# Two feed forwards' openings: an order each for ScalarE and VectorE, and low halves moved from GpSimd to VectorE

## The chip, the cores and the metric

The kernel runs on one core of a Trainium2 chip. The metric is the device time of one execution in microseconds; before, the median of three runs is 1371.8 us.

## The reference

Two transformer blocks run one after the other on 512 tokens of width 1024, in fp32. Each ends with a gated feed forward of inner width 2816, and the change concerns these two alone:

```python
# block 1
x = x + rms_norm(mixed, norm_mix_post)
h = rms_norm(x, norm_ffn_pre)
f = (silu(h @ w_gate) * (h @ w_up)) @ w_down
x = x + rms_norm(f, norm_ffn_post)
# block 2
x = x + merged @ w_out
h = rms_norm_2(x, norm_ffn)
x = x + (silu(h @ w_ffn_gate) * (h @ w_ffn_up)) @ w_ffn_down
```

`rms_norm(x, g)` is x / sqrt(mean(x²) + eps) * g over the 1024 columns of a token.

## The kernel before, in words

**Arithmetic.** TensorE multiplies in a reduced fp32 form, so each operand is split into a high and a low half, and a product takes three matmuls (`mm3`, or the three pairs in `prod`). A split is one ScalarE copy (the high half) and one subtraction (the low half), on VectorE or, where `split_from` is given `lo_eng`, on that engine. Splits of 1024 columns are made by `w8`, of 512 by `w4`; their results stand in the profile as `wt` and `u`.

**The feed forward.** `ffn` (L440) runs over 22 tiles of 128 inner columns. Per tile it takes products of quarter blocks in the manner of Strassen's scheme: instead of the four quarters of the tokens' matrix X and of the weights, it multiplies sums of them. The left sums of X (`s2`, `s3`, `p1`, `p4` and the quarter `a22`) are made once; the weights' sums are made in every tile by four GpSimd additions of 512 columns in place (`Tile.sums`, L397 to L400), on the raw tiles `G` (of w_gate) and `U` (of w_up) as they were loaded. From the sums come `wb` (the split of `U`) and `wa` (of `G`).

**An opening.** The left sums need the last two token tiles, which are not ready when the feed forward starts. So `ffn` first runs an opening: for the first 12 tiles of the first feed forward and the first 8 of the second ("heads"), it computes the gate products with the quarters that are there, `a11` (`first`) and `a12` (`second`). Its parts carry names: "L5" loads and splits tile 5's gate weights, "E5" copies out its first product (ScalarE), "S5" its silu (ScalarE). With these are woven, in the first feed forward, the norms of the token tiles 2 and 3 (`norm_fill`, "sq2", "rs2", "post2", "add2", "sq'2", "rs'2", "pre2", and the same with 3; "rs" is a reciprocal root of nine VectorE instructions, "sq" and "sq'" mean squares on ScalarE), then the left sums' subtractions, "sub0" and "sub1" (four VectorE subtractions of 512 columns each), and ten left blocks, "b0" to "b9": four TensorE transposes, two ScalarE high halves and two VectorE low halves, which the profile shows as `sh<-tp`. Two PSUM buffers take the transposes, so the third block waits for the first to be split. Within a tile's norm, `pre` writes what the left blocks transpose. Behind the opening stands the loop over all 22 tiles, whose first products are with `s2`.

**What sets the order.** The instructions of the parts are recorded by `noted` in `bag`; a string of names (`ORDER1` at L1062, `ORDER2` at L1388) then chains each engine's instructions in the order of the names through `behind` (L289), one string for both engines. TensorE is chained by `prod` and `left_block` as the code is written. Behind the chain, L527 splits the first tile's sums: high halves of `wb` and `wa` on ScalarE, low halves on GpSimd (they are the `wt` instructions of L255 on POOL). Then tile 1 is loaded, and its sums and tile 2's follow on GpSimd. All weights are loaded by SP into rotating raw buffers; two of these hold tile 0's `G` and `U` during the opening.

`early` counts the tiles whose gate weights are split by two `w4` instead of one `w8`: 2 in the first feed forward, 0 in the second.

Of the kernel before, what the change touches and what calls it, by code (L numbers as in the profile page):

```python
# [10 lines left out]
BF16 = mybir.dt.bfloat16  # L11
# [6 lines left out]
P = 128  # L18
S = 512
D = 1024  # L20
# [14 lines left out]
def transformer_pair(ctx: ExitStack, tc: tile.TileContext, A: dict, out: bass.AP, spill: dict):  # L35
# [6 lines left out]
    nc = tc.nc  # L42
# [20 lines left out]
    vec, sca = Engine(nc.vector, "dve"), Engine(nc.scalar, "act")  # L63
    bag = {}

    @contextmanager
    def noted(name):
        bags.append(bag.setdefault(name, []))
        yield
        bags.pop()  # L70
# [5 lines left out]
    wt1 = ctx.enter_context(tc.tile_pool(name="wt1", bufs=4))  # L76
# [6 lines left out]
    pl = {}  # L83
# [14 lines left out]
    cnt = [0, 0, 0, 0, 0]  # L98
    loads = []

    def nm(s):
        cnt[0] += 1
        return f"{s}_{cnt[0]}"
# [4 lines left out]
    def t_tile(shape, dt=F32):  # L108
        return pl["t"].tile(shape, dt, tag="t", name=nm("t"))

    def p_tile(shape, dt=F32):
        return pl["p"].tile(shape, dt, tag="p", name=nm("p"))

    def s_tile(n, tag, dt=F32, bufs=6):
        return sm.tile([P, n], dt, tag=tag, name=nm(tag), bufs=bufs)
# [12 lines left out]
    def tp_tile():  # L128
        return ps_tile("tp")
# [14 lines left out]
    def queue_after(later, earlier):  # L144

        tc.add_manual_dep(later.ins, earlier.ins.name,
                          mybir.DependencyInfo(mybir.DependencyClass.NoSync, mybir.DependencyReason.DATA),
                          reason="order")
# [38 lines left out]
            vec.scalar_tensor_tensor(y, t, 1.5, y, op0=ALU.subtract, op1=ALU.mult)  # L187
        return y

    def mean_square(x_ap):  # L190

        junk = (p_tile([P, D], BF16) if "p" in pl else t_tile([P, D], BF16) if "j" not in pl else
                pl["j"].tile([P, D], BF16, tag="j", name=nm("j")))
        ms = s_tile(1, "ms")
        sca.activation(junk, x_ap, AF.Square, scale=1.0 / 32.0, accum_out=ms)
        return ms
# [79 lines left out]
    def w8(src, pool, lo_eng=None):  # L276

        w = pool.tile([P, 2, 1024], F32R, tag="wt", name=nm("wt"))
        split_from(src, w[:, 0], w[:, 1], lo_eng=lo_eng)
        return w  # L280
# [8 lines left out]
    def behind(eng, ins):  # L289

        if eng in queue:
            queue_after(ins, queue[eng])
        queue[eng] = ins
        return ins
# [145 lines left out]
    def ffn(X, wgate, wup, wdown, t0, heads, early, h, order, before_last, second_phase, evac, middle):  # L440
# [14 lines left out]
        both = pl["raws"]  # L455
# [39 lines left out]
        for f in range(heads + 1):  # L495
# [22 lines left out]
            for n in (2 * i, 2 * i + 1):  # L518
                if i >= 0:
                    with noted(f"b{n}"):  # L520
                        late[n]()
        for name in order.split():
            for eng, ins in bag[name]:
                behind(eng, ins)
        bag.clear()
        pl["raws"], cnt[4] = both, 1
        t0.wb, t0.wa = w8(t0.U, wt1, nc.gpsimd), w8(t0.G, wt1, nc.gpsimd)  # L527
        T[1].load()
        T[1].w22 = w4(T[1].U[:, 512:1024])
        T[1].sums()  # L530
# [3 lines left out]
        for f in range(NF):  # L534
            t = T[f]
            n1, n2 = T[f + 1] if f + 1 < NF else None, T[f + 2] if f + 2 < NF else None
            p = n1 if n1 and not n1.head else None
# [104 lines left out]
    x_t = []  # L642
# [67 lines left out]
    for tt in range(NT):  # L710
# [4 lines left out]
        sq = t_tile([P, 2, 64])  # L715
# [12 lines left out]
    for tt in range(NT):  # L728
# [3 lines left out]
        pt = tp_tile()  # L732
# [201 lines left out]
    mixed = {}  # L934
# [31 lines left out]
    def norm_fill(tt):  # L966
        if tt == 0:
            rows[0] = (row_in("norm_mix_post"), row_in("norm_ffn_pre"))
        post_norm_then_pre(vec, mixed[tt], x_t[tt], *rows[0], mean_square, rsqrt, lambda n: noted(f"{n}{tt}"))

    hX = {}

# [5 lines left out]
    rows = [None]  # L978
# [50 lines left out]
    t0 = early_tile(A["w_gate"], A["w_up"])  # L1029
# [28 lines left out]
    def middle1():  # L1058
        hT2.extend(new_hT())
        flush()  # L1060

    ORDER1 = ("L2 L3 sq2 E0 rs2 E1 S0 post2 L4 add2 sq'2 E2 S1 sq3 L5 E3 S2 rs'2 rs3 L6 E4 S3 pre2 post3 L7 E5 S4 "  # L1062
              "add3 sq'3 L8 E6 S5 sub0 L9 E7 S6 rs'3 pre3 L10 E8 S7 b0 b1 sub1 L11 E9 S8 b2 b3 E10 S9 b4 b5 "
              "E11 S10 b6 b7 S11 b8 b9")
    ffn(hX, A["w_gate"], A["w_up"], A["w_down"], t0, 12, 2, mixed, ORDER1, [], down_phase1, evac1, (10, middle1))
    hT = hT2


# [190 lines left out]
    def gate_fill(_):  # L1259
# [3 lines left out]
    order = [[(U, 0)], [(U, 1), (G, 0)], [(Y, 0), (G, 0)], [(U, 2), (Y, 1)],  # L1263
             [(U, 3), (G, 0)], [(Y, 2), (G, 0)], [(G, 0), (Y, 3)], [(G, 0)]]
# [32 lines left out]
    for f2 in range(4):  # L1297
        wb = load_w(A["w_branch_b"][f2])
        for fi in range(2):
            f = 2 * f2 + fi  # L1300
# [16 lines left out]
    t0 = early_tile(A["w_ffn_gate"], A["w_ffn_up"])  # L1317
    hX = left_tiles()
# [30 lines left out]
    x_t = []  # L1349
# [33 lines left out]
    def load_x2():  # L1383
        for tt in (0, 1):
            x_t.append(u_tile([P, D]))
            nc.sync.dma_start(out=x_t[tt], in_=spill["x3"][tt])

    ORDER2 = ("L0 L1 L2 add3 sq3 rs3 E0 pre3 L3 E1 S0 L4 E2 S1 sub0 L5 E3 S2 L6 E4 S3 b0 b1 sub1 L7 E5 S4 b2 b3 "  # L1388
              "E6 S5 b4 b5 E7 S6 b6 b7 S7 b8 b9")
    ffn(hX, A["w_ffn_gate"], A["w_ffn_up"], A["w_ffn_down"], t0, 8, 0, h_t, ORDER2, [load_x2],  # L1390
        down_phase2, evac2, (10, middle2))
    hT = hT3
# [15 lines left out]
    for tt in range(NT):  # L1408
# [17 lines left out]
        n = len(parts) - 1  # L1426
# [15 lines left out]
def post_norm_then_pre(vec, m, xt, g_post, g_pre, mean_square, rsqrt, noted):  # L1442

    with noted("sq"):
        ms = mean_square(m)
    with noted("rs"):
        r = rsqrt(ms, 1)
    with noted("post"):
        vec.scalar_tensor_tensor(m, m, r, g_post, op0=ALU.mult, op1=ALU.mult)
    with noted("add"):  # L1450
        vec.tensor_tensor(xt, xt, m, op=ALU.add)
    with noted("sq'"):
        ms = mean_square(xt)
    with noted("rs'"):
        r2 = rsqrt(ms, 1)
    with noted("pre"):
        scale_rows(vec, m, xt, r2, g_pre)
# [121 lines left out]
```

## Time and profile before

| what | value |
|---|---|
| median of three runs (lowest, highest) | 1371.8 us (1370.57, 1372.34) |
| profiled execution, its own time | 1370.37 us |
| profiled execution, span | 1368.7 us |
| mean granted TensorE clock | 0.993 |
| TensorE busy | 1300.0 us (95%) |
| VectorE busy | 988.0 us (72%) |
| ScalarE busy | 733.2 us (54%) |
| GpSimd busy | 378.9 us (28%) |
| first opening | 229.2 to 289.2 us |
| second opening | 942.7 to 976.3 us |

The span runs from the first to the last instruction in the trace; the execution's own time is 1.7 us longer. Times in the views count from the span's start. Busy shares are means over the whole span and tell little of an opening, which has to be read in order of time. In the trace the operations of parts recorded by `noted` all have the line of the helper, L57, so they are told apart by tile and shape. A matmul's end is modelled, and the starts of two groups in a row give the better measure of how long one took.

### The profile page before, as it was taken

To read this page: it belongs to the slowest core of one execution; us is meant where nothing else is said; L and a number is where in the kernel's file an instruction comes from. 1 tells how busy PE (TensorE), PEld (TensorE's weight loads), DVE (VectorE), ACT (ScalarE), POOL (GpSimd) and SP (SyncE) were. 2 spreads that over 40 slices of the span, in tenths; PEclk is the share of its full clock that TensorE was granted. 3 is DMA by queue.
4 is the path that set the end of the run, shared out by engine and by line. 5 is a ranking of instruction groups with operands and counts; after the bars stand their busy time and mean duration, and the time that the engine had idled before them with its cause. 6 is when DMAs were issued, how large, how long until landed. Compare 5 with 4: busy or idle time off the path is not lost.

```text
span 1368.7 us, 20850 instructions
## 1 busy us (share of the span) xinstructions
PE 1300.0 (95%) x7724; PEld 1108.6 (81%) x7724; DVE 988.0 (72%) x1837; ACT 733.2 (54%) x1333; POOL 378.9 (28%) x367
## 2 busy tenths in 40 slices
PE   8989999789999999999998999989899999999997
PEld 6756667778889999787766778869889999998876
DVE  5889677778887765866886673656788766767665
ACT  6578876634444554544866564534544544544453
POOL 1433222145544341000233010210554344330002
PEclk9999999999999999999999999999999999999999
DMA  8214133434444433833121435553344334437441
GB/s 281 84 32 143 43 106 111 139 119 144 139 139 139 139 109 117 315 126 112 62 78 54 126 133 181 188 212 127 109 151 154 116 117 138 123 108 259 144 138 61
DMA packets 56309, 181.81 MB, mean 133 GB/s; under 512 B 8592, under 2 KB 8976, under 8 KB 56208
## 3 DMA queue, kind: packets, MB, share of 16 engines
q1 hardware_dynamic: 56064, 180.49, 40.2%
q8 instruction: 60, 0.98, 0.3%
q14 instruction: 41, 0.34, 0.1%
q10 hardware_dynamic: 144, 0.00, 0.0%
HBM read 167.88 MB, written 12.58 MB: 132 GB/s over the span
## 4 chain that ended last, share of the span: by engine, by line
PE 61%; DVE 20%; issue 9%; ACT 4%; DMA 3%; POOL 2%; SPq 0%; DVEq 0%; POOLq 0%; ACTq 0%
PE f L349 14%; PE tp L349 9%; PE f L168 5%; PE f L166 5%; PE f L167 5%; DVE t L363 3%; PE acc L166 3%; PE acc L168 3%; PE acc L167 3%; DVE u L363 2%; DVE wt L161 2%; DVE wt L363 1%; PE av L852 1%; DVE p L1196 1%; DVE u L57 1%
## 5 line engine op out<-in xcount | busy, mean ns | idle before, releaser
L349 PE MATMUL tp<-sh,wt 128*128 128x256 f32 x1584 | 205.3, 284 | 3.6 <-DVE sh L57 2.0
L349 PEld LDWEIGHTS tp<-sh,wt 128*128 128x128 f32 x1584 | 197.9, 192 | 11.2 <-DVE t L363 6.4
L360 ACT ACTIVATE wt<-raw 128x1024 fp32r<-128x1024 f32 x152 | 155.6, 1050 | 82.8 <-issue 66.7
L363 DVE TENSOR_TENSOR wt<-raw,wt 128x1024 fp32r<-128x1024 f32 x152 | 190.8, 1255 | 2.0 <-ACT wt L360 1.9
L161 DVE TENSOR_TENSOR wt<-raw,wt 128x1024 fp32r<-128x1024 f32 (+1 forms) x88 | 109.7, 1251 | 50.2 <-ACT wt L160 49.1
L397 POOL TENSOR_TENSOR raw<-raw,raw 128x512 f32<-128x512 f32 x44 | 63.8, 1450 | 289.8 <-DVE wt L363 171.4
L166 PE MATMUL f<-wt,u 128*128 128x512 f32 x280 | 112.2, 402 | 3.9 <-ACT wt L254 2.2
L168 PE MATMUL f<-wt,u 128*128 128x512 f32 x280 | 112.2, 401 | 2.0 <-DVE u L255 2.0
L160 ACT ACTIVATE wt<-raw 128x1024 fp32r<-128x1024 f32 (+1 forms) x88 | 91.3, 1045 | 42.5 <-PE f L168 13.0
L167 PE MATMUL f<-wt,u 128*128 128x512 f32 x280 | 111.3, 398 | 1.4 <-DVE wt L255 1.0
L166 PE MATMUL f<-u,wt 128*128 128x512 f32 x272 | 107.5, 395 | 0.3 <-ACT nx L1097 0.2
L167 PE MATMUL f<-u,wt 128*128 128x512 f32 x272 | 107.0, 393 | 0.0
L168 PE MATMUL f<-u,wt 128*128 128x512 f32 x272 | 106.8, 393 | 0.0
L349 PE MATMUL f<-u,wt 128*128 128x256 f32 x720 | 98.3, 287 | 0.5 <-DVE wt L57 0.5
L349 PEld LDWEIGHTS f<-u,wt 128*128 128x128 f32 x720 | 92.5, 196 | 0.7 <-DVE wt L57 0.7
L363 DVE TENSOR_TENSOR u<-tp,u 128x256 f32<-128x256 f32 x88 | 36.6, 416 | 72.8 <-PE tp L349 72.8
L399 POOL TENSOR_TENSOR raw<-raw,raw 128x512 f32<-128x512 f32 x44 | 57.1, 1297 | 83.9 <-DVE u L363 73.7
L349 PE MATMUL f<-sh,u 128*128 128x256 f32 x528 | 72.0, 286 | 5.0 <-DVE t L363 5.0
L254 ACT ACTIVATE wt<-raw 128x1024 fp32r<-128x1024 f32 x48 | 49.7, 1055 | 45.1 <-PE acc L168 22.0
L349 PEld LDWEIGHTS f<-sh,u 128*128 128x128 f32 x528 | 66.2, 191 | 7.8 <-DVE t L363 7.8
L349 PE MATMUL f<-sh,wt 128*128 128x256 f32 x528 | 70.5, 283 | 0.0
L360 ACT ACTIVATE u<-u 128x256 f32<-128x256 f32 x44 | 18.4, 417 | 95.4 <-DVE u L363 95.4
(335 smaller groups left out, 3043.5 us busy)
## 6 DMA issues: line engine op xcount, KB each, us to landing
raw<-in_w_down SPq DMA_DIRECT2D x44, 512.0 KB, 3.9
raw<-in_w_ffn_down SPq DMA_DIRECT2D x44, 512.0 KB, 4.1
raw<-in_w_gate SPq DMA_DIRECT2D x34, 512.0 KB, 4.1
raw<-in_w_ffn_gate SPq DMA_DIRECT2D x30, 512.0 KB, 4.3
raw<-in_w_out SPq DMA_DIRECT2D x24, 512.0 KB, 3.6
raw<-in_w_up SPq DMA_DIRECT2D x22, 512.0 KB, 3.8
raw<-in_w_ffn_up SPq DMA_DIRECT2D x22, 512.0 KB, 4.0
raw<-in_w_in SPq DMA_DIRECT2D x11, 512.0 KB, 5.0
```

What stands on the lines that cost most here:

```text
L57: i = fn(*a, **kw)
L160: sca.activation(w[:, 0, c], raw[:, c], AF.Copy)
L161: pl["lo"].tensor_tensor(w[:, 1, c], raw[:, c], w[:, 0, c].bitcast(F32), op=ALU.subtract)
L166: nc.tensor.matmul(ps, lhsT=st[0], rhs=mv[0], start=first, stop=False)
L167: nc.tensor.matmul(ps, lhsT=st[0], rhs=mv[1], start=False, stop=False)
L168: nc.tensor.matmul(ps, lhsT=st[1], rhs=mv[0], start=False, stop=last)
L254: sca.activation(hi, src, AF.Copy)
L349: i = nc.tensor.matmul(ps[:, :256], lhsT=st[a], rhs=mv[b], start=first and k == 0 and n == 0, stop=k == 3 and n == 2, skip_group_check=True)
L360: return behind("act", nc.scalar.activation(out, src, fn))
L363: return behind("dve", nc.vector.tensor_tensor(out, a, b, op=op))
L397: add(G[:, lo], G[:, lo], U[:, lo], op=ALU.add)
L399: add(U[:, hi], G[:, lo], U[:, hi], op=ALU.add)
```

## The change

The order becomes a pair of strings, one that chains ScalarE and one that chains VectorE, each with its own sequence. The two splits of the first sums become parts of their own, "W" (`wb`) and "A" (`wa`); their low halves go to VectorE, and their places are in the orders, W between the last left blocks, A at the end. In ScalarE's order A's high half stands ahead of blocks 8 and 9. In the first feed forward `early` becomes 1, and the mean squares of token tile 3 write their unused result into a buffer of another pool, "pt".

```diff
-    def mean_square(x_ap):
+    def mean_square(x_ap, pool=None):
...
-        for name in order.split():
-            for eng, ins in bag[name]:
-                behind(eng, ins)
+        pl["raws"], cnt[4] = both, 1
+        with noted("W"):
+            t0.wb = w8(t0.U, wt1)
+        with noted("A"):
+            t0.wa = w8(t0.G, wt1)
+        for eng, names in zip(("act", "dve"), order):
+            for name in names.split():
+                for e, ins in bag[name]:
+                    if e == eng:
+                        behind(eng, ins)
         bag.clear()
-        pl["raws"], cnt[4] = both, 1
-        t0.wb, t0.wa = w8(t0.U, wt1, nc.gpsimd), w8(t0.G, wt1, nc.gpsimd)
         T[1].load()
...
-        post_norm_then_pre(vec, mixed[tt], x_t[tt], *rows[0], mean_square, rsqrt, lambda n: noted(f"{n}{tt}"))
+        post_norm_then_pre(vec, mixed[tt], x_t[tt], *rows[0],
+                            lambda a: mean_square(a, "pt" if tt == 3 else None), rsqrt, lambda n: noted(f"{n}{tt}"))
...
-    ORDER1 = ("L2 L3 sq2 E0 rs2 E1 S0 post2 L4 add2 sq'2 E2 S1 sq3 L5 E3 S2 rs'2 rs3 L6 E4 S3 pre2 post3 L7 E5 S4 "
-              "add3 sq'3 L8 E6 S5 sub0 L9 E7 S6 rs'3 pre3 L10 E8 S7 b0 b1 sub1 L11 E9 S8 b2 b3 E10 S9 b4 b5 "
-              "E11 S10 b6 b7 S11 b8 b9")
-    ffn(hX, A["w_gate"], A["w_up"], A["w_down"], t0, 12, 2, mixed, ORDER1, [], down_phase1, evac1, (10, middle1))
+    ORDER1 = ("L1 L2 L3 E0 sq2 E1 S0 L4 E2 S1 L5 sq'2 E3 sq3 S2 E4 L6 S3 E5 L7 S4 E6 L8 S5 L9 E7 S6 sq'3 E8 L10 S7 "
+              "b0 b1 L11 E9 S8 b2 b3 E10 S9 b4 b5 W E11 S10 b6 b7 S11 A b8 b9",
+              "L1 L2 rs2 post2 L3 add2 L4 rs'2 L5 rs3 L6 pre2 L7 post3 add3 L8 sub0 L9 rs'3 L10 pre3 b0 b1 L11 "
+              "b2 b3 sub1 b4 b5 b6 b7 W b8 b9 A")
+    ffn(hX, A["w_gate"], A["w_up"], A["w_down"], t0, 12, 1, mixed, ORDER1, [], down_phase1, evac1, (10, middle1))
...
-    ORDER2 = ("L0 L1 L2 add3 sq3 rs3 E0 pre3 L3 E1 S0 L4 E2 S1 sub0 L5 E3 S2 L6 E4 S3 b0 b1 sub1 L7 E5 S4 b2 b3 "
-              "E6 S5 b4 b5 E7 S6 b6 b7 S7 b8 b9")
+    ORDER2 = ("L0 L1 L2 sq3 E0 L3 E1 S0 L4 E2 S1 L5 E3 S2 L6 E4 S3 b0 b1 L7 E5 S4 b2 b3 E6 S5 b4 b5 W E7 S6 b6 b7 "
+              "S7 A b8 b9",
+              "L0 L1 L2 add3 rs3 pre3 L3 L4 sub0 L5 L6 b0 b1 sub1 L7 b2 b3 b4 b5 b6 b7 W b8 b9 A")
```

**GpSimd at the end of the first opening.** The names are raw weight tiles; wt_3332 and wt_3335 are the low halves of the first tile's `wb` and `wa`. Before:

```order
L397 TENSOR_TENSOR raw_3338<-raw_3338,raw_3340 128x512
L398 TENSOR_TENSOR raw_3340<-raw_3340 128x512
L255 TENSOR_TENSOR wt_3332<-raw_2718,wt_3332 128x1024
L255 TENSOR_TENSOR wt_3335<-raw_2717,wt_3335 128x1024
L399 TENSOR_TENSOR raw_3340<-raw_3338,raw_3340 128x512
L400 TENSOR_TENSOR raw_3338<-raw_3340,raw_3338 128x512
L397 TENSOR_TENSOR raw_3349<-raw_3349,raw_3351 128x512
L398 TENSOR_TENSOR raw_3351<-raw_3351 128x512
```

With the change:

```order
L397 TENSOR_TENSOR raw_3335<-raw_3335,raw_3337 128x512
L398 TENSOR_TENSOR raw_3337<-raw_3337 128x512
L397 TENSOR_TENSOR raw_3346<-raw_3346,raw_3348 128x512
L398 TENSOR_TENSOR raw_3348<-raw_3348 128x512
L399 TENSOR_TENSOR raw_3337<-raw_3335,raw_3337 128x512
L400 TENSOR_TENSOR raw_3335<-raw_3337,raw_3335 128x512
L399 TENSOR_TENSOR raw_3348<-raw_3346,raw_3348 128x512
L400 TENSOR_TENSOR raw_3346<-raw_3348,raw_3346 128x512
```

The two rows of L255 are gone, and tile 2's first two sums stand directly behind tile 1's.

**ScalarE in the middle of the first opening.** `wt<-raw` rows are gate weights' high halves, `u<-f` and `u<-acc` copies and silus of products, and the row that writes `ms_2783` is the mean square "sq'3" of token tile 3, which waits for VectorE's addition. Before:

```order
L57 ACTIVATE wt_3065<-raw_3063 128x1024
L57 ACTIVATE u_2836<-f_2998 128x256
L57 ACTIVATE u_2836<-acc_2966 128x256
L57 ACTIVATE p_2782,ms_2783<-x_297 128x1024
L57 ACTIVATE wt_3097<-raw_3095 128x1024
L57 ACTIVATE u_2837<-acc_3030 128x256
L57 ACTIVATE u_2836<-f_2998 128x256
L57 ACTIVATE wt_3153<-raw_3151 128x1024
L57 ACTIVATE u_2837<-f_3068 128x256
```

With the change:

```order
L57 ACTIVATE wt_3062<-raw_3060 128x1024
L57 ACTIVATE u_2836<-acc_2963 128x256
L57 ACTIVATE u_2837<-acc_3027 128x256
L57 ACTIVATE wt_3094<-raw_3092 128x1024
L57 ACTIVATE u_2836<-f_2995 128x256
L57 ACTIVATE wt_3150<-raw_3148 128x1024
L57 ACTIVATE u_2837<-f_3065 128x256
L57 ACTIVATE u_2837<-acc_3027 128x256
L57 ACTIVATE pt_2782,ms_2783<-x_297 128x1024
```

The mean square stands two weight halves later: ahead of the high halves of L8 and L9 before, behind both now.

**VectorE at the end of the first opening.** `sh<-tp` rows are left blocks' low halves; rows of `u_3127` (before) and `u_3124` (now) are two of the four subtractions of "sub1". Before:

```order
L57 TENSOR_TENSOR sh_2830<-tp_3142,sh_2830 128x2x128
L57 TENSOR_TENSOR sh_2831<-tp_3142,sh_2831 128x2x128
L57 TENSOR_TENSOR u_3127<-u_2159 128x512
L57 TENSOR_TENSOR u_3127<-u_1518,u_3127 128x512
L57 TENSOR_TENSOR u_3128<-u_1518,u_2159 128x512
L57 TENSOR_TENSOR u_3128<-u_1518,u_3127 128x512
```

With the change, from the same blocks on:

```order
L57 TENSOR_TENSOR sh_2830<-tp_3139,sh_2830 128x2x128
L57 TENSOR_TENSOR sh_2831<-tp_3139,sh_2831 128x2x128
L57 TENSOR_TENSOR wt_3250<-raw_3248,wt_3250 128x1024
L57 TENSOR_TENSOR sh_2826<-tp_3180,sh_2826 128x2x128
L57 TENSOR_TENSOR sh_2827<-tp_3180,sh_2827 128x2x128
L57 TENSOR_TENSOR sh_2824<-tp_3189,sh_2824 128x2x128
L57 TENSOR_TENSOR sh_2825<-tp_3189,sh_2825 128x2x128
L57 TENSOR_TENSOR u_3124<-u_2159 128x512
```

And the opening's last rows with the change:

```order
L57 TENSOR_TENSOR wt_3329<-raw_2718,wt_3329 128x1024
L57 TENSOR_TENSOR sh_2824<-tp_3311,sh_2824 128x2x128
L57 TENSOR_TENSOR sh_2825<-tp_3311,sh_2825 128x2x128
L57 TENSOR_TENSOR sh_2832<-tp_3320,sh_2832 128x2x128
L57 TENSOR_TENSOR sh_2833<-tp_3320,sh_2833 128x2x128
L57 TENSOR_TENSOR wt_3332<-raw_2717,wt_3332 128x1024
L363 TENSOR_TENSOR u_2834<-tp_3358,u_2834 128x256
```

"sub1" has moved behind tile 11's low half and the blocks 2 and 3, and the low halves of `wb` (wt_3329) and `wa` (wt_3332) are VectorE's now, ahead of and behind the last two blocks.

## Rows read from the trace of the kernel before

**Rows 1.** The page, busy us (share of the span) xinstructions of each engine.
```profile
PE 1300.0 (95%) x7724; PEld 1108.6 (81%) x7724; DVE 988.0 (72%) x1837; ACT 733.2 (54%) x1333; POOL 378.9 (28%) x367
```

**Rows 2.** Stretches: busy us (x) of PE, PEld, DVE, ACT, POOL; clock, DMA, GB/s.
```profile
229.20:289.20 60.00, 43.58 (x329) 41.34 (x328) 45.17 (x89) 31.34 (x67) 13.49 (x8) 0.94 0.37 123
230.00:260.00 30.00, 22.86 (x180) 21.63 (x180) 21.31 (x46) 17.16 (x33) 0.00 (x0) 1.00 0.40 135
270.00:280.00 10.00, 3.23 (x23) 3.05 (x23) 9.80 (x9) 2.94 (x8) 6.25 (x4) 0.84 0.28 81
960.00:970.00 10.00, 6.67 (x45) 6.50 (x44) 9.20 (x13) 5.43 (x13) 5.36 (x4) 0.83 0.32 105
```

**Rows 3.** TensorE in time, first opening: start, us, operation, count, [idle before <-releaser].
```profile
233.25 0.50 PE L349 MATMUL f<-u,u 128*128 128x256 f32 x2 [2.42 <-DVE rs_t L57]
...
246.86 1.60 PE L349 MATMUL f<-u,wt 128*128 128x256 f32 x12
248.30 1.84 PE L349 MATMUL acc<-u,wt 128*128 128x256 f32 x14
...
267.75 1.29 PE L316 MATMUL tp<-ident,u 128*128 128x128 f32 x8 [1.48 <-DVE sh L57]
...
278.69 1.94 PE L316 MATMUL tp<-ident,u 128*128 128x128 f32 x8 [6.77 <-DVE sh L57]
...
289.23 2.99 PE L349 MATMUL tp<-sh,wt 128*128 128x256 f32 x23 [1.03 <-DVE sh L57]
```

**Rows 4.** VectorE in time, first opening.
```profile
232.47 0.14 DVE L57 TENSOR_SCALAR rs_a<-ms 128x1 f32<-128x1 f32 x1
...
235.41 1.28 DVE L57 SCALAR_TENSOR_TENSOR u<-u,rs_y,row 128x1024 f32<-128x1024 f32 x1
...
258.82 0.68 DVE L57 TENSOR_TENSOR u<-u 128x512 f32<-128x512 f32 x1
259.54 1.90 DVE L57 TENSOR_TENSOR u<-u,u 128x512 f32<-128x512 f32 x3
261.35 1.22 DVE L57 TENSOR_TENSOR wt<-raw,wt 128x1024 fp32r<-128x1024 f32 x1
262.49 0.15 DVE L57 TENSOR_SCALAR rs_a<-ms 128x1 f32<-128x1 f32 x1
...
264.39 1.42 DVE L57 SCALAR_TENSOR_TENSOR u<-x,rs_y,row 128x512 f32<-128x512 f32 x2
...
268.18 1.34 DVE L57 TENSOR_TENSOR u<-u 128x512 f32<-128x512 f32 x1
269.56 7.18 DVE L57 TENSOR_TENSOR u<-u,u 128x512 f32<-128x512 f32 x3
```

**Rows 5.** GpSimd in time, end of the first opening.
```profile
267.70 1.27 POOL L397 TENSOR_TENSOR raw<-raw,raw 128x512 f32<-128x512 f32 x1 [42.50 <-DVE sh L57]
...
270.64 5.55 POOL L255 TENSOR_TENSOR wt<-raw,wt 128x1024 fp32r<-128x1024 f32 x2
```

**Rows 6.** ScalarE in time, end of the first opening.
```profile
265.84 0.94 ACT L57 ACTIVATE sh<-tp 128x256 fp32r<-128x256 f32 x3 [2.38 <-DVE u L57]
...
268.96 1.06 ACT L254 ACTIVATE wt<-raw 128x1024 fp32r<-128x1024 f32 x1
```

**Rows 7.** TensorE in time, second opening.
```profile
955.62 1.04 PE L316 MATMUL tp<-ident,u 128*128 128x128 f32 x8
...
959.36 1.04 PE L316 MATMUL tp<-ident,u 128*128 128x128 f32 x8
...
966.59 1.94 PE L316 MATMUL tp<-ident,u 128*128 128x128 f32 x8 [3.33 <-DVE sh L57]
...
971.79 1.03 PE L316 MATMUL tp<-ident,u 128*128 128x128 f32 x8
...
976.33 3.10 PE L349 MATMUL tp<-sh,wt 128*128 128x256 f32 x24 [1.01 <-DVE sh L57]
```

**Rows 8.** VectorE in time, second opening, one subtraction.
```profile
961.16 2.88 DVE L57 TENSOR_TENSOR u<-u,u 128x512 f32<-128x512 f32 x1
```

More of the change, by code (lines that the diff above doesn't have):

```diff
@@ L188, in rsqrt @@
         return y
-    def mean_square(x_ap):
-        junk = (p_tile([P, D], BF16) if "p" in pl else t_tile([P, D], BF16) if "j" not in pl else
+    def mean_square(x_ap, pool=None):
+        junk = pl[pool].tile([P, D], BF16, tag=pool, name=nm(pool)) if pool else (p_tile([P, D], BF16) if "p" in pl else t_tile([P, D], BF16) if "j" not in pl else
                 pl["j"].tile([P, D], BF16, tag="j", name=nm("j")))
```

## The prediction

> **What bounds the kernel now.** Read the busy line first [rows 1]: TensorE is busy for 95% of the span, so an opening of a feed forward can give back only the holes that it leaves in TensorE and the time in which its clock is low. Then cut the span into stretches [rows 2]. The first opening lasts from 229.2 to 289.2 us and holds 43.58 us of TensorE work; the rest, some 16 us, is holes. Its clock is 0.94 there on the mean: 1.00 from 230 to 260, then 0.84 from 270 to 280, that is, part of the time at the lower of its two levels (1.2 GHz against 2.4). The stretch from 960 to 970 in the second opening shows 0.83.
>
> The order of TensorE in time [rows 3] shows where the holes are. The largest is 6.77 us ahead of 278.69 and ends on a VectorE low half ("sh"). VectorE in the same stretch [rows 4] shows why: three subtractions that took 1.90 us from 259.54 took 7.18 us from 269.56. GpSimd [rows 5] was then working on the first sums' low halves, two of them in 5.55 us, and the two engines took turns: each subtraction waited for the GpSimd instruction in progress. Ahead of this, VectorE had come late to the third token tile's last norm step (264.39), and the high halves of the first left blocks waited for it [rows 6]; the third left block came at 267.75. The second opening has the same picture, smaller [rows 7, 8]: one subtraction stretched to 2.88, a hole of 3.33, a low clock behind it.
>
> **The change, part by part.**
>
> *First opening, up to left blocks 2 and 3.* The single order held ScalarE and VectorE to one string; now VectorE has its own, and ScalarE's high halves run ahead. I take it that VectorE then never waits for a high half. Its chain from 232.47 [rows 4] to the end of the norm of tile 3 is: four reciprocal roots at 1.90 (262.49 to 264.39) = 7.60; two post scalings at 1.28 = 2.56; the two additions and the low halves L3 to L10, ten at 1.14 (261.35 to 262.49; an addition has the shape of a low half) = 11.40; two pre scalings at 1.42 = 2.84; one set of subtractions, 258.82 to 261.35 = 2.53. Sum 26.93, so the norm of tile 3 ends at 259.4, where it now ends at 264.39 + 1.42 = 265.8. From there blocks 0 and 1 still need their three high halves (0.94 [rows 6]) and the last low half behind them, an estimate of 1.4 together; the row is 267.75 - 265.8 = 1.94, with a low half of 1.14 standing in between that has now moved ahead. So blocks 2 and 3 come at 260.8 instead of 267.75.
>
> Can TensorE be there by then? From 229.2 it has 17 products at 1.44 (246.86 to 248.30 [rows 3]), two blocks and two products more (3.74, 955.62 to 959.36 [rows 7]): 257.5 without any hole. Tile 1's weights now take one split instead of two, and its low half stands ahead of the norm, so the 2.42 hole at 233.25 should go. VectorE sets the time, and TensorE waits up to 3.3 us there.
>
> *First opening, to its end.* Two rounds of two blocks and two products at full clock, 2 x 3.74 = 7.48, then the last stretch, 4.54 (971.79 to 976.33 [rows 7]), give 260.8 + 7.48 + 4.54 = 272.8. The second set of subtractions no longer meets the two GpSimd low halves. Two costs come on top. The high half of A now stands on ScalarE ahead of blocks 8 and 9, whose low halves the loop waits for: between 0 (it fits the wait for the transposes) and 1.06, its own duration [rows 6]; I take 0.9, since ScalarE's last silu ends only as block 8's transposes run. And the sums of tile 1 move up into VectorE's chain, because GpSimd has no low halves ahead of them. The row for such a meeting is 268.18: a subtraction of 0.68's worth (258.82) took 1.34 while GpSimd's first sum ran [rows 4, 5], 0.66 lost. Bounds: 0 if the sums miss the chain, 1.32 if two sums each cost an instruction that much; I take 0.66. The Trainium skill, "SBUF — State Buffer", section "Who interferes with whom", puts it harder: VectorE with two SBUF inputs and GpSimd reading SBUF exclude each other for a whole instruction, whoever starts first. By that rule each of the two moved low halves, and the tile 3 norm, could each lose a whole sum of 1.27 instead of 0.66, and the total gain below would be some 2 us smaller; the trace agrees with the exclusion (the subtraction from 268.18 ended only after the sum did), and leaves open which instructions will meet.
>
> The loop starts at 272.8 + 0.9 + 0.66 = 274.4 instead of 289.23 [rows 3]: **14.8 us less**.
>
> *Second opening.* The subtraction of 2.88 [rows 8] goes back to 0.68, so the hole of 3.33 becomes 1.1: 2.2 less. The clock then should not fall: 966.59 to 971.79 took 5.20 for the work that 955.62 to 959.36 did in 3.74 [rows 7], so 1.46 less. The high half of A costs the same 0.9. Sum: **2.8 us less**.
>
> *Costed at nothing.* The low halves W and A on VectorE are two more of 1.22 in each opening. W stands behind block 7, where VectorE waits for transposes; A stands behind block 9, where VectorE waits for the loop's first product. Without that cover each would cost up to its 1.22 once per opening, 4.9 in all. ScalarE's instructions keep their number but for one split. On SP, the load of w_up for tile 2 moves ahead of the first w_down, which in turn waits for W's low half because it takes that buffer; the instructions queued behind it are the loop's own loads. The spill of token tile 2 goes ahead of one w_gate load, and nothing waits for a spill here. The first w_down is needed only when the loop's first tile is done, so I cost this at nothing; if it is late, the price is that of its lateness once per opening.
>
> **Sum:** 14.8 + 2.8 = 17.6. The profiled execution took 1370.37 in all with a span of 1368.7; it becomes 1352.8 and 1351.1. The median of the three runs shown, 1371.8, is 1.4 above the profiled one; against it the forecast is 1371.8 - 17.6 = **1354.2 us**.
>
> **Rivals.**
>
> *B. The clock falls at new holes.* Holes still stand ahead of blocks 2 and 3 (up to 3.3) and the loop's start. For it: the hole of 3.33 was followed by the low clock [rows 2, 7]. Against it: 2.42 was not (1.00 from 230 to 260), and the hole is 3.3 only if TensorE had none before. The price of one such fall is 1.46 in the second opening, and in the first (278.69 to 289.23 = 10.54 against 3.74 + 4.54) 2.26. One of the larger size gives 1354.2 + 2.3 = 1356.5. The chain of VectorE having small gaps would come to about the same.
>
> *C. The new orders bring nothing, only GpSimd's low halves count.* Loads or some other wait hold the first opening's middle as now, and blocks 2 and 3 stay at 267.75. Then the hole of 6.77 and its low clock, 2.26, go, less the 0.9 of A: 8.1, and 2.8 in the second opening: 10.9, 1360.9 us. For it: VectorE has a few waits for high halves only, and the loads of the gate weights have buffers that come free with low halves. Against it: the 26.93 of work is less than the 33.3 that it took.
>
> *D. Slower.* The loop settles into another phase: its loads come in another order, GpSimd's sums fall upon VectorE's low halves, and TensorE waits for these in every tile. The two feed forwards have 22 tiles each, 44 in all. At the row's 0.66 a tile that is 29 us against 17.6 gained: 1383 us. It decides from 17.6 / 44 = 0.40 a tile on. Against it: each tile's loads wait for buffers that the tile before frees, which brings the order of the loop back whatever its start.
>
> *E. The change doesn't do what it says.* The order lists fix what each engine does next, but not when; if the loop's start is set by a load (w_down or tile 2's weights), what the opening wins is waited for there: 1371.8.
>
> **How the numbers follow.** Forecast 0.55, B 0.25, C 0.12, D 0.04, E 0.04. A measurement of this kernel tells about 0.2% (2.7 us) from no change, so the first three are faster: 0.92; the same 0.04, slower 0.04. The low end is the forecast without the cost of A and the sums' meetings in both openings, 2 x 0.9 + 0.66 = 2.5, and a little more where the products come sooner: 1351. The high end takes in B, the harder meetings and most of C: 1361.5.
>
> **What would show it.** In the profile after: blocks 2 and 3 of the first opening near 261, no wait of over 3.5 us in TensorE in either opening, a clock of 1.00 in both, no subtraction of over 2 us on VectorE, the loop starting 45 us after the opening's start instead of 60, and 31 instead of 33.6 in the second; W's and A's low halves on VectorE with nobody waiting for them. A first opening of over 50 us with full-size gaps in VectorE would be C; a main loop whose tiles take over 0.4 us longer would be D.

## The result, and the profile after

The changed kernel takes 1355.09 us (median of 4 runs, 1354.03 to 1355.67) against 1372.07 us for the kernel before in the same comparison. The ratio is 0.9881, with a 95% interval from 0.9869 to 0.9894: 17.0 us faster, where 17.6 were forecast (1354.2 us). Two slow executions are left out of all times and ratios: one of 1785.92 us of e5_a_last_w_early, at a mean granted clock of 0.655, and one of 6496.49 us of the kernel before, beside the runs e1 to e4.

The stretches of the changed kernel first, to be held against [rows 2]; the columns are the same (busy us of PE, PEld, DVE, ACT, POOL, granted clock, DMA share, GB/s).

```profile
230.00:276.00 46.00, 41.50 (x330) 40.51 (x329) 41.46 (x90) 30.71 (x66) 8.24 (x6) 0.96 0.42 137
230.00:260.00 30.00, 28.67 (x237) 28.27 (x235) 28.39 (x63) 18.97 (x36) 0.75 (x1) 1.00 0.55 176
262.00:267.00 5.00, 5.00 (x30) 5.00 (x31) 4.97 (x9) 1.88 (x7) 0.41 (x1) 0.66 0.33 108
276.00:280.00 4.00, 4.00 (x22) 4.00 (x23) 3.07 (x5) 2.97 (x4) 0.00 (x0) 0.57 0.73 224
929.70:960.90 31.20, 28.11 (x234) 27.33 (x232) 24.39 (x46) 21.66 (x48) 8.04 (x6) 1.00 0.32 106
961.00:966.70 5.70, 5.70 (x36) 5.70 (x37) 4.63 (x8) 2.94 (x4) 0.00 (x0) 0.70 0.70 218
```

The first opening is 46 us long instead of 60, with nearly the same TensorE busy time in it, 41.50 us for 43.58: the holes are what went, from 16.4 us to 4.5. VectorE is busy for 28.39 of the 30 us from 230 to 260, where it had 21.31. The clock is 1.00 up to 260, and then low in three places: from 262 to 267, and at the start of both loops (276 to 280, 961 to 967). The second opening keeps its full clock.

TensorE in order of time in the changed kernel, first opening and then the second (columns as in [rows 3]):

```profile
230.01 1.60 PE L349 MATMUL acc<-u,u 128*128 128x256 f32 x12
231.44 1.62 PE L349 MATMUL f<-u,wt 128*128 128x256 f32 x12
...
261.34 1.29 PE L316 MATMUL tp<-ident,u 128*128 128x128 f32 x8 [2.67 <-DVE sh L57]
262.39 2.68 PE L349 MATMUL acc<-u,wt 128*128 128x256 f32 x12
264.87 2.13 PE L349 MATMUL av<-u,wt 128*128 128x256 f32 x12
266.84 1.04 PE L316 MATMUL tp<-ident,u 128*128 128x128 f32 x8
...
270.58 1.04 PE L316 MATMUL tp<-ident,u 128*128 128x128 f32 x8
...
275.89 4.61 PE L349 MATMUL tp<-sh,wt 128*128 128x256 f32 x24 [1.79 <-DVE sh L57]
```
```profile
951.54 1.29 PE L316 MATMUL tp<-ident,u 128*128 128x128 f32 x8 [1.25 <-DVE sh L57]
...
960.86 4.24 PE L349 MATMUL tp<-sh,wt 128*128 128x256 f32 x24 [1.81 <-DVE sh L57]
```

The opening now starts at 230.01, not 229.24, so places are compared by their distance from its start. The wait of 2.42 at the second product is gone (231.44 follows without one). Blocks 2 and 3 come 31.3 us after the start (261.34 - 230.01), before 38.5; their wait is 2.67, behind which two products took 2.48 and 1.97 between starts instead of 1.5: the low clock. Block 4 (266.84) waits for nothing where it waited 6.77. The loop starts 45.9 us after the opening, with a wait of 1.79 that was 1.03 [rows 3]. The second opening has a wait of 1.25 where it had 3.33, is 31.2 us long instead of 33.7, and has the same longer wait at its end, 1.81 for 1.01 [rows 7].

VectorE in the first opening of the changed kernel, which answers to [rows 4]:

```profile
233.22 0.14 DVE L57 TENSOR_SCALAR rs_a<-ms 128x1 f32<-128x1 f32 x1
...
258.53 1.41 DVE L57 SCALAR_TENSOR_TENSOR u<-x,rs_y,row 128x512 f32<-128x512 f32 x2
...
261.88 1.62 DVE L57 TENSOR_TENSOR wt<-raw,wt 128x1024 fp32r<-128x1024 f32 x1
...
264.75 0.67 DVE L57 TENSOR_TENSOR u<-u 128x512 f32<-128x512 f32 x1
265.46 1.90 DVE L57 TENSOR_TENSOR u<-u,u 128x512 f32<-128x512 f32 x3
...
273.24 1.77 DVE L57 TENSOR_TENSOR wt<-raw,wt 128x1024 fp32r<-128x1024 f32 x1
274.99 1.42 DVE L57 TENSOR_TENSOR sh<-tp,sh 128x256 fp32r<-128x256 f32 x4
276.32 1.22 DVE L57 TENSOR_TENSOR wt<-raw,wt 128x1024 fp32r<-128x1024 f32 x1
```

From 233.22 (the first root) to the end of the norm of tile 3 (258.53 + 1.41 = 259.94) are 26.72 us, against a chain of 26.93 worked out ahead. The second set of subtractions is back at 1.90 where it took 7.18. L11's low half took 1.62 and W's 1.77 instead of the 1.22 that A's took (276.32), beside GpSimd's sums:

```profile
259.25 1.80 POOL L397 TENSOR_TENSOR raw<-raw,raw 128x512 f32<-128x512 f32 x1 [33.32 <-DMA raw<-in_w_up]
261.14 1.28 POOL L398 TENSOR_TENSOR raw<-raw 128x512 f32<-128x512 f32 x1
...
272.65 1.28 POOL L400 TENSOR_TENSOR raw<-raw,raw 128x512 f32<-128x512 f32 x1
```

The first of tile 1's sums took 1.80 instead of 1.27 [rows 5]: here GpSimd waited for VectorE's norm, not VectorE for GpSimd. The second sum (261.14) had begun when L11's low half came, and there VectorE waited.

### The profile page after: what moved, and what is told of

Its sections match the earlier page's. It is cut to its first block, busy times and chain, and to the rows that moved or that the text cites. A ratio compares the mean times of both kernels' runs of the same rounds, so it can differ in the third digit from the quotient of the medians.

```text
span 1354.0 us, 20845 instructions
## 1 busy us (share of the span) xinstructions
PE 1298.9 (96%) x7724; PEld 1109.6 (82%) x7724; DVE 983.5 (73%) x1840; ACT 733.4 (54%) x1332; POOL 367.8 (27%) x363
## 4 chain that ended last, share of the span: by engine, by line
PE 54%; DVE 13%; issue 7%; ACT 3%; DMA 2%; POOL 1%; SPq 0%; DVEq 0%; POOLq 0%; ACTq 0%
PE f L349 14%; PE tp L349 10%; PE f L166 4%; PE f L168 4%; PE f L167 4%; DVE t L363 4%; PE acc L166 3%; PE acc L167 3%; PE acc L168 3%; DVE u L363 2%; DVE wt L363 1%; DVE p L1203 1%; DVE wt L161 1%; PE acc L349 1%; PE av L168 1%
## 5 line engine op out<-in xcount | busy, mean ns | idle before, releaser
L360 ACT ACTIVATE wt<-raw 128x1024 fp32r<-128x1024 f32 x152 | 155.6, 1051 | 85.6 <-issue 66.5
L254 ACT ACTIVATE wt<-raw 128x1024 fp32r<-128x1024 f32 x44 | 45.5, 1058 | 44.1 <-PE acc L168 24.5
```

Source lines behind the costliest of these rows:

```text
L254: sca.activation(hi, src, AF.Copy)
L360: return behind("act", nc.scalar.activation(out, src, fn))
```

## The experiments

All openings are measured from their first product to the first product of the loop, by the starts in each profile; a first tile from there to the second tile's first product. "Blocks 2, 3" is counted from the opening's start. The times come from groups of runs on different chips: beside e1 to e4 the kernel before took 1370.97 us, beside e5, e6, e7 and e9 1372.03, beside e8 and e10 1372.6 (one run). The other columns are from one profiled execution each.

| kernel | time, us | blocks 2, 3 | opening 1 | first tile 1 | opening 2 | first tile 2 |
|---|---|---|---|---|---|---|
| before | 1372.07 | 38.5 | 59.99 | 14.89 | 33.66 | 14.87 |
| the change | 1355.09 | 31.3 | 45.88 | 16.37 | 31.16 | 16.15 |
| e1_lows_only | 1361.89 | 40.7 | 54.24 | 15.00 | 30.22 | 14.98 |
| e2_orders_only | 1360.24 | 31.4 | 49.62 | 14.88 | 33.76 | 14.89 |
| e3_a_last | 1354.76 | 31.4 | 45.41 | 14.81 | 30.45 | 14.91 |
| e4_l10_late | 1354.87 | 30.3 | 46.06 | 16.34 | 30.99 | 14.87 |
| e5_a_last_w_early | 1353.39 | 31.4 | 45.00 | 14.91 | 30.37 | 15.00 |
| e6_all | 1354.09 | 30.3 | 46.49 | 16.31 | 30.37 | 14.73 |
| e9_l11_late | 1353.3 | 30.3 | 45.25 | 15.08 | 30.39 | 15.02 |
| e7_change_again | 1354.91 | 31.4 | 45.10 | 14.90 | 31.06 | 14.89 |
| e10_short_root | 1352.32 (one run) | 29.9 | 43.22 | 14.88 | 31.23 | 14.89 |
| e8_p_junk | 1359.36 (one run) | 31.4 | 46.94 | 16.31 | 31.11 | 14.88 |

Between the openings nothing moved with any of these edits: the first loop behind its first tile, up to its last tile's first product, took 236.01 us before and 236.38 with the change, the second 243.77 and 243.74. The lengths of opening 1 can't be compared without a look at the clock: from block 2 to block 4 TensorE took 4.00 us in e7_change_again at full clock, and at a lower one 5.50 in the change, 5.06 in e3_a_last, 5.34 in e5_a_last_w_early and 6.50 in e8_p_junk.

### One part at a time

**e1_lows_only**, the kernel before with the two low halves on VectorE in the old single order:

```diff
-        t0.wb, t0.wa = w8(t0.U, wt1, nc.gpsimd), w8(t0.G, wt1, nc.gpsimd)
+        with noted("W"):
+            t0.wb = w8(t0.U, wt1)
+        with noted("A"):
+            t0.wa = w8(t0.G, wt1)
...
-              "E11 S10 b6 b7 S11 b8 b9")
+              "W E11 S10 b6 b7 S11 b8 b9 A")
...
-              "E6 S5 b4 b5 E7 S6 b6 b7 S7 b8 b9")
+              "E6 S5 b4 b5 W E7 S6 b6 b7 S7 b8 b9 A")
```

> The kernel before with one part of the change: the low halves of W and A go to VectorE, in the old single order (W behind block 5, A behind block 9). Theory (each part of the change brings a piece of its own): blocks 2 and 3 stay near 267.7, the hole of 6.77 ahead of block 4 and the 2.26 of low clock behind it go, in the second opening 2.2 and 1.46: 12.7 less, 1359 us. Rival 1 (GpSimd's two low halves were the whole cause, the new orders bring nothing): about 1355, as the change. Rival 2 (the orders were all): about 1372.

Measured: 1361.89 us, ratio 0.994 (0.9925 to 0.9954). TensorE and VectorE around the blocks of its first opening:

```profile
234.91 0.50 PE L349 MATMUL f<-u,u 128*128 128x256 f32 x2 [2.42 <-DVE rs_t L57]
...
260.87 5.49 PE L349 MATMUL acc<-u,wt 128*128 128x256 f32 x24 [2.14 <-ACT u L57]
...
276.61 1.29 PE L316 MATMUL tp<-ident,u 128*128 128x128 f32 x8 [1.12 <-DVE sh L57]
...
285.14 3.11 PE L349 MATMUL tp<-sh,wt 128*128 128x256 f32 x24 [1.01 <-DVE sh L57]
```
```profile
271.09 0.68 DVE L57 TENSOR_TENSOR u<-u 128x512 f32<-128x512 f32 x1
271.81 2.86 DVE L57 TENSOR_TENSOR u<-u,u 128x512 f32<-128x512 f32 x3
```

The wait of 6.77 is down to 1.12 and the loop's start has its old 1.01, as the theory had it. The waits of 2.42 and 2.14 in the opening's middle have stayed, and here both were followed by a low clock. Behind the first, 22 matmuls took 4.24 us (235.63 to 239.87) that took 2.73 before; behind the second, 24 took 5.3 us (260.87 to 266.16) that took 2.97 before:

```profile
235.60:239.90 4.30, 4.26 (x23) 4.26 (x24) 2.60 (x7) 1.67 (x2) 0.00 (x0) 0.60 0.34 122
261.00:267.00 6.00, 6.00 (x29) 6.00 (x30) 5.72 (x14) 3.03 (x6) 0.00 (x0) 0.52 0.40 123
```

That is 3.8 us of low clock. Part of it is taken back because nothing waits ahead of blocks 2 and 3 any more (1.48 before), so these come 2.2 us later than in the kernel before. With the 1.12 that is left ahead of block 4 this is most of what is missing: the two openings gave 9.2 us (5.75 and 3.44) where 12.7 were expected. The second opening is 30.22 long: all of its gain, and more than the change's, comes from this part.

**e2_orders_only**, the change with the low halves on GpSimd as before; W and A are out of both orders.

```diff
-        with noted("W"):
-            t0.wb = w8(t0.U, wt1)
-        with noted("A"):
-            t0.wa = w8(t0.G, wt1)
...
         bag.clear()
+        t0.wb, t0.wa = w8(t0.U, wt1, nc.gpsimd), w8(t0.G, wt1, nc.gpsimd)
```

> The change without the move: the pair of orders stands, the low halves of W and A stay on GpSimd as before. Theory: blocks 2 and 3 come near 261.3 as with the change; then one GpSimd low half of 2.8 meets the second set of subtractions and holds blocks 4 and 5 by 2 to 4 us in the first opening, by 2.2 and a low clock in the second; the loops start without A's high half ahead of blocks 8 and 9: 1357 to 1360 us. Rival 1 (the orders bring nothing): 1372. Rival 2 (the orders were all): 1355 or less.

Measured: 1360.24 us, ratio 0.9923 (0.9908 to 0.9938).

```profile
261.78 1.29 PE L316 MATMUL tp<-ident,u 128*128 128x128 f32 x8 [2.68 <-DVE sh L57]
...
268.55 0.63 PE L316 MATMUL tp<-ident,u 128*128 128x128 f32 x4 [2.17 <-DVE u L57]
...
273.71 1.70 PE L316 MATMUL tp<-ident,u 128*128 128x128 f32 x8 [1.66 <-DVE sh L57]
...
280.04 3.11 PE L349 MATMUL tp<-sh,wt 128*128 128x256 f32 x24 [1.19 <-DVE sh L57]
```
```profile
264.96 0.68 DVE L57 TENSOR_TENSOR u<-u 128x512 f32<-128x512 f32 x1
265.67 7.23 DVE L57 TENSOR_TENSOR u<-u,u 128x512 f32<-128x512 f32 x3
...
264.96 2.90 POOL L255 TENSOR_TENSOR wt<-raw,wt 128x1024 fp32r<-128x1024 f32 x1
```

Blocks 2 and 3 come at 31.4 us after the start, as with the change: this is the orders' part (with tile 1's single split and the other pool, which this kernel has too). The subtractions take 7.23 beside GpSimd's low halves again, now ahead of blocks 5 to 7 (2.17 and 1.66). The second opening is as long as before (33.76 against 33.66): there the orders bring nothing. So both single-cause rivals fall. In the first opening the orders take 10.4 us off (59.99 to 49.62), the low halves 5.8 (54.24), both together 14.1 or, by e7_change_again, 14.9; they overlap, and e1_lows_only has 3.8 of low clock in it. In the second the low halves take 3.4, the orders nothing.

### What the change leaves

**e3_a_last** moves A's high half behind the last blocks.

```diff
-              "b0 b1 L11 E9 S8 b2 b3 E10 S9 b4 b5 W E11 S10 b6 b7 S11 A b8 b9",
+              "b0 b1 L11 E9 S8 b2 b3 E10 S9 b4 b5 W E11 S10 b6 b7 S11 b8 b9 A",
...
-              "S7 A b8 b9",
+              "S7 b8 b9 A",
```

> The change with A's high half behind blocks 8 and 9 on ScalarE instead of ahead of them, nothing else. Theory: the wait at the loop's start falls from 1.8 to about 1.0 in both openings and the clock no longer falls behind it (it cost 1.5 in each loop's first tile): 0.8 + 1.5 twice, 4.6 less than the change, about 1350.5 us. Rival: A's low half then comes too late for the third product of the loop, the wait moves there, and the time stays at 1355.

Measured: 1354.76 us, ratio 0.9889 (0.987 to 0.9907), no difference from the change that the runs can tell; the 4.6 us expected did not come. Where the first loop starts:

```profile
277.15 3.10 PE L349 MATMUL tp<-sh,wt 128*128 128x256 f32 x24 [1.71 <-DVE sh L57]
```
```profile
273.25 1.42 DVE L57 TENSOR_TENSOR sh<-tp,sh 128x256 fp32r<-128x256 f32 x4 [0.72 <-ACT sh L57]
274.58 1.76 DVE L57 TENSOR_TENSOR wt<-raw,wt 128x1024 fp32r<-128x1024 f32 x1
```

In the second opening the wait at the loop's start fell from 1.81 to 1.17; in the first it stayed at 1.71. There W's low half, stretched to 1.76 by GpSimd's sums, stood ahead of block 8's. Both first tiles took 14.8 to 14.9 here, as forecast; what that was worth is shown by e7_change_again.

**e5_a_last_w_early** moves W's low half as well (the cut shows the edit against e3_a_last).

```diff
-              "b2 b3 sub1 b4 b5 b6 b7 W b8 b9 A")
+              "b2 b3 sub1 b4 b5 W b6 b7 b8 b9 A")
...
-              "L0 L1 L2 add3 rs3 pre3 L3 L4 sub0 L5 L6 b0 b1 sub1 L7 b2 b3 b4 b5 b6 b7 W b8 b9 A")
+              "L0 L1 L2 add3 rs3 pre3 L3 L4 sub0 L5 L6 b0 b1 sub1 L7 b2 b3 b4 b5 W b6 b7 b8 b9 A")
```

> The change with A's high half behind blocks 8 and 9 on ScalarE, as in e3_a_last, and W's low half ahead of blocks 6 and 7 on VectorE instead of behind them, in both openings. Theory (in e3_a_last the loop still waited 1.7 because W's low half, 1.76 long beside GpSimd's sums, stood ahead of block 8's low half): the wait at the first loop's start falls from 1.7 to 1.0, both openings end 0.1 to 0.7 earlier than in e3_a_last (45.4 and 30.5 us long there), the first tiles of both loops take 14.9: about 1350 us. Rival: the early W meets the sums of tile 2 and holds blocks 6 and 7, so the openings stay at 45.4 and 30.5.

```profile
273.76 1.22 PE L316 MATMUL tp<-ident,u 128*128 128x128 f32 x8
275.99 3.11 PE L349 MATMUL tp<-sh,wt 128*128 128x256 f32 x24 [1.01 <-DVE sh L57]
```

The wait is 1.01, as in the kernel before; from the last blocks to the loop the first opening takes 2.23 (273.76 to 275.99), where the change took 3.01 (272.88 to 275.89), and the second opening is 30.37 long, 0.8 shorter than the change's. That is 1.6 us in all, and in the times it can't be told from the spread: 1353.39 (three runs, 1352.52 to 1355.64), ratio 0.9863 (0.9847 to 0.988), beside 0.9871 (0.9855 to 0.9888) for the change on the same chip. The 1350 us expected here and in e6_all were not reached.

**e4_l10_late** shortens VectorE's chain ahead of block 2 by one low half; **e6_all** is that on e5_a_last_w_early, and **e9_l11_late** moves the next low half back too.

```diff
-              "L1 L2 rs2 post2 L3 add2 L4 rs'2 L5 rs3 L6 pre2 L7 post3 add3 L8 sub0 L9 rs'3 L10 pre3 b0 b1 L11 "
+              "L1 L2 rs2 post2 L3 add2 L4 rs'2 L5 rs3 L6 pre2 L7 post3 add3 L8 sub0 L9 rs'3 pre3 b0 b1 L10 L11 "
```

and, from e6_all to e9_l11_late:

```diff
-              "L1 L2 rs2 post2 L3 add2 L4 rs'2 L5 rs3 L6 pre2 L7 post3 add3 L8 sub0 L9 rs'3 pre3 b0 b1 L10 L11 "
-              "b2 b3 sub1 b4 b5 W b6 b7 b8 b9 A")
+              "L1 L2 rs2 post2 L3 add2 L4 rs'2 L5 rs3 L6 pre2 L7 post3 add3 L8 sub0 L9 rs'3 pre3 b0 b1 L10 "
+              "b2 b3 sub1 L11 b4 b5 W b6 b7 b8 b9 A")
```

> The change with the low half of L10 moved on VectorE from ahead of the norm of tile 3 to behind blocks 0 and 1 (first opening only). Theory (VectorE's chain up to the end of that norm sets when blocks 2 and 3 come): these come 1.1 us earlier, the hole of 2.67 shrinks to about 1.5 and the low clock behind it (1.7 us) goes or shrinks; the product with L10 waits some 0.5: 1352.5 to 1354.5 us. Rival (TensorE only waits for L10 in place of the blocks): 1355.

> e5_a_last_w_early and the low half of L10 behind blocks 0 and 1, as in e4_l10_late. Theory: as in e4_l10_late the blocks 2 and 3 come 1 us earlier and block 5 then waits about 1.4 for the second set of subtractions, because VectorE's work up to there is the same: the first opening as long as in e5_a_last_w_early within 0.5, about 1350 us. Rival (the low clock behind the wait ahead of block 2 is what costs): 1.5 less.

> e6_all with the low half of L11 behind the second set of subtractions on VectorE. Theory (VectorE is full from the opening's start to block 5, so that whatever stands last ahead of it is waited for): the wait ahead of block 5 goes, a wait of about 1 comes ahead of the product with L11, the first opening is as long as in e6_all within 0.5. Rival: the product with L11 has 1.4 of slack more than block 5, and the opening is 1 us shorter.

```profile
259.97 1.29 PE L316 MATMUL tp<-ident,u 128*128 128x128 f32 x8 [1.64 <-DVE sh L57]
...
261.68 1.46 PE L349 MATMUL acc<-u,wt 128*128 128x256 f32 x10 [0.18 <-DVE wt L57]
...
266.65 0.63 PE L316 MATMUL tp<-ident,u 128*128 128x128 f32 x4 [1.36 <-DVE u L57]
```
```profile
260.40 3.45 DVE L57 TENSOR_TENSOR wt<-raw,wt 128x1024 fp32r<-128x1024 f32 x2
```

In e4_l10_late blocks 2 and 3 come 1.0 us earlier, with a wait of 1.64 for 2.67. But block 5 then waits 1.36 for the second set of subtractions, and the opening is 46.06 long, not shorter. Part of that wait is a meeting with GpSimd: the low halves of L10 and L11, now side by side with tile 1's sums, took 3.45 us together where two alone take 2.36 (1.14 to the next start and 1.22), and block 5 stands 0.7 later than in e7_change_again (37.0 us after the start for 36.3). In e9_l11_late the subtractions are in time and the two products wait, 1.16 and 0.98. Whatever stands last on VectorE is waited for. In e6_all the product with L10 waits 1.11 and the clock falls there and at the loop's start, so its 46.49 says little of the edit, and that e9_l11_late is 1.2 shorter does not speak for the rival. The times, 1354.87, 1354.09 (0.9851 to 0.9881) and 1353.3 (0.9844 to 0.9876), are not told apart from the change's.

**e10_short_root** takes work off VectorE alone: the third Newton step of the four roots is left out. In this code each step also turns the sign of the root (it computes `(t - 1.5) * y`), so with two steps the four roots are not only less exact but negative: only the run's times are of use.

```diff
-        for _ in range(3):
+        for _ in range(steps):
...
+                           lambda m, n: rsqrt(m, n, steps=2 if tt > 1 else 3),
```

> The change with two instead of three Newton steps in the four reciprocal roots of token tiles 2 and 3 in the first opening (the third step is left out there, so these four roots are less exact). It takes some 4 x 0.45 = 1.8 off VectorE's chain and nothing off any other engine. Theory (VectorE's chain sets blocks 2 and 3): these come 29.5 instead of 31.3 us after the opening's start, and the first opening takes 43.3 to 44 instead of 45.1 to 45.9. Rival (TensorE, ScalarE or a load is as late as VectorE): 31 and over 45.

```profile
260.12 1.29 PE L316 MATMUL tp<-ident,u 128*128 128x128 f32 x8 [1.47 <-DVE sh L57]
...
273.44 3.10 PE L349 MATMUL tp<-sh,wt 128*128 128x256 f32 x24 [1.91 <-DVE sh L57]
```
```profile
240.06 0.15 DVE L57 TENSOR_SCALAR rs_a<-ms 128x1 f32<-128x1 f32 x1 [0.47 <-ACT p L57]
...
260.65 1.23 DVE L57 TENSOR_TENSOR wt<-raw,wt 128x1024 fp32r<-128x1024 f32 x1
```

Blocks 2 and 3 come at 29.9 and the opening is 43.22 long, 1.9 less than the shorter of the two executions of the change. Both that execution (e7_change_again) and this one ran at full clock here. Of the 1.9, 1.5 stands at blocks 2 and 3 and is the chain's: it is the bound. The other 0.4 lies between blocks 2 and 6: L11's low half took 1.23 here (260.65), not 1.62 beside GpSimd's sum, and the wait of 0.36 ahead of block 5 that e7_change_again has is not there. The 29.5 was missed by 0.4 because another wait appeared: VectorE now waited 0.47 for a mean square on ScalarE (240.06).

**e8_p_junk** puts the unused result of tile 3's mean squares back into the pool of before.

```diff
-lambda a: mean_square(a, "pt" if tt == 3 else None)
+lambda a: mean_square(a, None)
```

> The change with the unused result of token tile 3's mean squares in the pool of before again. Theory: nothing changes, since the pool's buffers are free by then: blocks 2 and 3 at 31.3, first opening 45.1 to 45.9. Rival: the mean square waits for a buffer and VectorE's roots wait for it: over 46.5.

Blocks 2 and 3 stayed at 31.4 us, so the pool costs nothing. The opening is 46.94 long, which by its length alone would speak for the rival; but the wait ahead of block 2 was the same 2.7, and behind it the clock was low:

```profile
263.00:269.00 6.00, 6.00 (x30) 6.00 (x29) 5.69 (x10) 2.48 (x8) 1.32 (x2) 0.52 0.26 91
```

From block 2 to block 4 it took 6.50 us, where e7_change_again took 4.00. The length is the clock's doing, not the pool's; of its 1359.36 us, one run, no more can be said.

### The clock

**e7_change_again** is the changed kernel once more.

> The changed kernel itself, on the same chip as the three others, to compare them with: 1355 us, first opening 45.9 us long, first tiles of the loops 16.2 to 16.4. If these first tiles take 14.9 here, the low clock behind the loop's start is an accident of one execution and not a consequence of A's place.

```profile
230.60:275.70 45.10, 40.13 (x329) 38.94 (x328) 41.77 (x89) 30.83 (x66) 8.54 (x6) 1.00 0.43 140
262.00:267.00 5.00, 4.60 (x37) 4.19 (x38) 4.95 (x10) 3.23 (x11) 1.05 (x1) 1.00 0.37 111
276.00:280.00 4.00, 4.00 (x36) 4.00 (x35) 3.94 (x6) 2.67 (x4) 0.00 (x0) 1.00 0.75 236
```

The waits are the same (2.7 ahead of block 2, 1.92 and 1.79 at the loops' starts), and the clock is 1.00 in all these stretches. With the products behind block 3 faster, TensorE now reaches block 5 ahead of VectorE's second set of subtractions:

```profile
266.93 0.63 PE L316 MATMUL tp<-ident,u 128*128 128x128 f32 x4 [0.36 <-DVE u L57]
```

The loops have first tiles of 14.90 and 14.89, where the profile of the result had 16.37 and 16.15. So the low clock is no fixed consequence of A's place, as e3_a_last expected; it differs between executions of one program. It may still be a matter of odds: in the five profiles with A ahead of block 8, 4 of 10 first tiles took over 16 us; in the seven others (with the kernel before), where the loop waited 1.0 to 1.7, 1 of 14 did. These are too few to tell. What A's and W's places cost for certain is the 0.8 us of waiting per opening. The repeat's median, 1354.91, equals the first one's within the spread.

## Why the prediction was right

**VectorE's chain and blocks 2 and 3: right.** Forecast 26.93 us and blocks 2 and 3 at 260.8, that is 31.6 after the opening's start; measured 26.72 and 31.3. e10_short_root and e4_l10_late show that this chain is the cause: shorter by 1.8 and 1.1, it brings the blocks 1.4 and 1.0 earlier. The second product's wait of 2.42 went with the orders and tile 1's single split, not with the low halves: it stands in e1_lows_only and not in e2_orders_only. Which of the two it was, no run tells.

**The end of the first opening: right, but two terms stand for something else.** Forecast 45.2 us, measured 45.88 and, without the low clock, 45.10 (e7_change_again). There the stretches are 31.36 to blocks 2 and 3 (forecast 31.6), 8.30 from there to block 6 (7.48 and the 0.66 for the sums) and 5.44 from there to the loop (4.54 and the 0.9 for A).

The 0.9 is not A's alone. The longer wait at the loop's start is 0.76 (1.79 for 1.03). In the second opening A's place explains it: W's low half took its 1.22 there, and moving A alone took the wait from 1.81 to 1.17. In the first, W's low half, costed at nothing, was stretched by GpSimd's sums and stood ahead of block 8: the wait was 1.79, 1.92 and 2.22 where W took 1.77, 1.97 and 2.27 (the change, e7_change_again, e4_l10_late), and with A moved it was still 1.71. e5_a_last_w_early, with both moved, returns the 0.76; W alone was not moved, so the two shares are not known.

The 0.66 for tile 1's sums did not arise at the norm. VectorE was first there, and GpSimd waited (1.80 for 1.27). One low half later GpSimd was first: L11 took 1.62, and in e7_change_again block 5 waited 0.36 for what follows it; in e10_short_root VectorE was first again, and the sum took 2.25. That agrees with the Trainium skill ("SBUF — State Buffer", "Who interferes with whom"), by which the shared ports are an exclusive lock and the order of issue decides who blocks. The prediction had taken from the same section that the gain could be some 2 us smaller. That much did not come: L11's meeting cost 0.4 (8.30 for the 7.89 of e10_short_root between blocks 2 and 6), and W's share at the loop's start overlaps with A's.

**The second opening: right.** 2.8 us forecast, 2.50 measured. The wait went from 3.33 to 1.25 (forecast 1.1), the clock stayed at 1.00.

**The rivals.** C (the orders bring nothing) is false in the first opening, where e2_orders_only has 10.4 us from them, and true in the second. B (a low clock behind the new waits) came to pass in the profiled execution, with 1.5 us in the opening (5.50 from block 2 to block 4, against 4.00), of which 0.9 is left at block 6 (9.24 against 8.30, since at full clock block 5 waits for VectorE), and 1.5 and 1.3 in the loops' first tiles, and not in e7_change_again; the price of one fall, 1.46 to 2.26, was of the right size, and it is an event of single executions. D and E fell: the loops behind their first tiles moved by 0.37 and -0.03 us.

**What the right total hides.** The openings gave 14.1 and 2.5 in the profiled execution, 16.6 together, and the loops' first tiles took 2.8 back. The spans differ by 14.7, since stretches that the change does not touch were not the same either (the first opening began 0.77 later, and from the first loop's last tile to the second opening it took 1.48 less). The medians differ by 17.0. A forecast from one profile can't be held to better than that. Two of the signs that the prediction named failed as well: the clock was not 1.00 throughout the first opening, and W's low half was waited for.

## What to carry to other kernels

Where two engines are chained to one list, each inherits the other's waits; with a list each, the engine with slack runs ahead, and the other is held up by its own work alone. When that can be reached is the sum of its own rows up to the point that is waited for. When a chain without gaps has become the bound, moving a step past the point that waits only names another step to wait for; it gets shorter by work taken off that engine (e10_short_root), or by a step moved to where the engine idles (W in e5_a_last_w_early). And when a low half or sum is moved between VectorE and GpSimd, look not at its length but at which instructions of the other engine it will run beside, and who waits for those.

## What the runs showed of the hardware that was not expected

The granted clock behind a wait of TensorE is not settled by the wait's length. A wait of 2.67 ahead of block 2 was followed by 0.66 in the profile of the result, by 1.00 in e7_change_again (the same program), and by 0.52 in e8_p_junk; e2_orders_only had 2.68 and kept 1.00. Waits of 2.42 and 2.14 were followed by 0.60 and 0.52 in e1_lows_only; in the kernel before the same waits, 2.42 and 2.13, left the clock at 1.00. Even a wait of 0.97, at the first loop's start in e6_all, was followed by a low clock (first tile 16.31). Each fall made the work behind it 1.1 to 2.5 us longer. Why one execution falls and another does not stays open: no run here tells it.
